# The first modulation of a seven-sublayer block, read and summed by quarters of channels, with the first sublayer's products between the quarters

## The chip, the cores and the metric

The kernel runs on one NeuronCore of a Trainium2 chip. The metric is the device time of one execution in microseconds (us). TensorE multiplies matrices, VectorE and ScalarE work on tiles, GpSimd (POOL) does a few fills and issues some transfers, SyncE (SP) issues most transfers. All arithmetic is in float32 in and out; products with weights are split into a high and a low part to keep that precision.

## The reference

One sequence of 256 tokens with 1024 channels goes through seven sublayers: for each of two layers a SwiGLU feed-forward, a mixer (mLSTM, then Mamba-2) and a second feed-forward, and at last a hybrid of block attention and short convolution. Each sublayer is modulated by a vector that is computed from a conditioning vector `c`:

```python
mod = silu(c) @ ada_w[i] + ada_b[i]            # 9 x 1024 columns per layer: shift, scale, gate of 3 sublayers
hmod = rms_norm(x, g_pre) * (1 + scale) + shift
y = rms_norm(fn(hmod), g_post)
x = x + weight * gate * y
fn = lambda h: (silu(h @ w1) * (h @ w3)) @ w2  # feed-forward, inner width 2816
```

## The kernel before

**Products.** A weight unit is a tile of 128 partitions by 1024 float32 (512 KB): two rows of blocks of 128 input channels by 512 columns, for instance. It is split on the chip: `hi` is the value rounded to the type fp32r (a copy, on ScalarE or VectorE), `lo = raw - hi` (VectorE). The modulated input is held the same way, channels on partitions, as XH and XL (8 blocks of 128 channels by 256 tokens). Each product is XH·hi + XH·lo + XL·hi, summed in PSUM. In feed-forward group 0 the input is the stationary operand and 512 weight columns move (`group_b` and `unit_b`, output tokens by columns); in groups 1 to 5 the weights are stationary and 256 tokens move (`proj_t`), and the products with w2 (`wide`) of a group follow one group later.

**The stream.** `Stream` is one ordered list of entries: weight units ("w"), rows of a modulation matrix ("ada"), sums and calls. `pump_dma` issues the loads of up to nine entries ahead of the oldest one still open (nine raw buffers), all on SyncE's queue. `step` takes the next entry: a weight unit is split into one of six hi/lo buffers; an ada entry (128 input channels by 1024 columns) is a multiply-add on VectorE, acc += raw * cs[:, k], with the conditioning value of each partition as scalar. After eight such rows the sum over partitions is taken on TensorE. Which ada entries stand between which weight units is written out in the tables GATE_AT, EARLY and COLS_AT at the top of the file, by position in a sublayer's plan (`plan_ffn`). `st.ahead` and `pieces` split some units ahead of their use. Engines run their instructions in program order.

**The start** (from the `prev = Tail(-1)` line on). ScalarE's queue loads the rows of c, the constants cC and the norm gains. SyncE's queue loads four ada rows, the first token tile of X, five ada rows, `rel` and `oh` (a small table of relative-position biases and its one-hot), then goes on with the stream; the second tile of X comes after step 5 of 8 pairs. The first modulation is 16 entries (8 blocks of k, shift and scale), 16 multiply-adds on `accC` of 128x2048, whose first row the bias `ada_b` was loaded into on POOL's queue. Between them the first token tile is normed (`x_root`, `scale_x`). Eight `bias_head` pairs (a matmul of 128x384 and a ScalarE copy into `st8`, 128 partitions wide) follow on TensorE. Then come the transposes of token tile 0 (`pre_tr`), sixteen column sums (`cols_sum`), the columns AB (`cols_set`: 1 + scale times the gain, and shift), the modulation (`affine`), and the split into XH and XL (`high`, `low`). The second token tile is normed here too, but transposed and modulated inside the first `group_b` (`between.transposes`, `between.second`), by the order list `orders[0]`. Then w1's and w3's group 0 are four units each.

`late_constants`, at position 12 of the first sublayer's plan, transposes some small rows and writes `st8` (1.5 MB) from the chip to a scratch tensor `rel_scr` in memory, which only the last sublayer reads.

Line 92 of the kernel is the helper through which every engine instruction passes, so nearly all rows carry L92 and are told apart by their tiles: accC the modulation's sums, raw the loaded tiles, hi and lo the split weights, pa the PSUM tiles of products, pb the bias heads, AB the columns, scr scratch tiles, cs the conditioning values, sil and gf the gated values of the feed-forward, py the PSUM tiles of w2.

Of the kernel before, what the change touches and what calls it, by code (L numbers as in the profile page):

```python
# [10 lines left out]
F32 = mybir.dt.float32  # L11
# [15 lines left out]
TR1_AT = 5  # L27
BY_ACT = (1, 2)
NEXT_CORE = 7
X1AT = 4  # L30
OHAT = 9

GATE_AT = [((3, 5, 7, 8), 9), ((1, 2, 3, 4), 4)] + 2 * [(range(4, 12), 11)] + [((4, 5, 6, 7), 8), (range(4, 12), 11)]
EARLY = {1: (range(12, 28, 2), 29), 4: (range(13, 29, 2), 29)}
MB_COLS = (list(range(2, 8)) + list(range(16, 26)), 26)
COLS_AT = [(range(11, 27, 2), 28), (range(5, 13), 12)] + 2 * [(range(13, 29), 29)] + [MB_COLS, (range(13, 29), 29)]


def bcast(row, n):
# [56 lines left out]
class Stream:  # L96
# [28 lines left out]
    def add_ada(self, src, info):  # L125
        self.entries.append(("ada", info, src, 1, 1024))

    def add_sum(self, srcs, fn):
# [9 lines left out]
    def pump_dma(self, n=RAW_BUFS):  # L138
        while self.dma < len(self.entries) and self.dma < min(self.open | {self.cur}) + n:
            kind, _, src, a, b = self.entries[self.dma]  # L140
            if kind in ("w", "ada"):
                raw = self.raw_pool.tile([128, 1024], F32, name="raw")
                self.nc.sync.dma_start(raw.rearrange("p (a b) -> p a b", a=a), src)
                self.raws[self.dma] = raw
            self.dma += 1

# [9 lines left out]
    def step(self, apart=False):  # L156

        if self.cur >= len(self.entries):
            return False
        kind, what, src, a, b = self.entries[self.cur]  # L160
        nc = self.nc
        self.pump_dma()
        if kind == "call":
            self.cur += 1
            what()
            return True
        raw = src if kind == "sum" else self.raws[self.cur]
        if kind == "ada":
# [82 lines left out]
def tile_blocks(ctx: ExitStack, tc, x, c, ada_w, ada_b, norm_pre, norm_post, ffn_w1, ffn_w3, ffn_w2,  # L251
# [125 lines left out]

    Gs, ABs = {}, {}

    def cols_sum(p, j):  # L380
        T.matmul(p[:, j:j + 96], accs[0][:, j * 128:(j + 1) * 128], ones[:, 0:96], start=True, stop=True)

    def cols_set(n, p):

        v = lambda t: t.rearrange("p (i h) -> p i h", h=2)
# [76 lines left out]
    def plan_hy():  # L462
# [10 lines left out]
    plans = [lambda: plan_ffn(0, 0), plan_ml, lambda: plan_ffn(0, 1), lambda: plan_ffn(1, 0),  # L473
             plan_mb, lambda: plan_ffn(1, 1), plan_hy]
# [11 lines left out]
    for n in range(n_sub):  # L486
# [15 lines left out]
    extra.setdefault(12, []).append(lambda: late_constants())  # L502
    at, last_unit = 0, {}
    for n in range(n_sub):
        for p in subs[n]:
# [200 lines left out]
            T.matmul(ps, x, w, start=first, stop=(last and kk == KT - 1 and i == len(ops) - 1))  # L706


    orders = [[(0, 1), (1, 1), (0, 6), (1, 6), (2, 1), (3, 1), (2, 6), (3, 6)]]
    orders += 7 * [[(i, 5) for i in range(4)] + [(i, 2) for i in range(4)]]  # L710

    def group_b(xh, xl, evac, between=None):

# [3 lines left out]
        if between is not None:  # L717
            for tok in range(2):
                ps = pa([128, 512])
                order = orders[-1] if tok else orders.pop(0)  # L720
                for j, (i, parts) in enumerate(order):
                    hi, lo = st.get(us[i])
                    unit_b(hi, lo, xh, xl, 2 * i, ps, tok, parts, j == len(order) - 1)
# [92 lines left out]
    def ffn(tail, between):  # L816
        with ExitStack() as es:
# [4 lines left out]
            for g in range(6):  # L822
# [5 lines left out]
                if g == 0:  # L828
                    flat = lambda t: t.rearrange("p (t c) s -> p t (c s)", t=2)
                    sb, gb = flat(sil), flat(gf)  # L830
                    group_b(XH, XL, lambda tok, p: A.activation(sb[:, tok], p, AF.Silu), between)
                    group_b(XH, XL, lambda tok, p: V.tensor_mul(gb[:, tok], p, sb[:, tok]))

                    def transposes(gb, gh, gl):
                        yield
# [768 lines left out]
    st8 = rc.tile([128, 8, 384], F32, name="st8")  # L1604
    with tc.tile_pool(name="pst", bufs=1, space=PSUM) as pst:
        crow0 = rc.tile([16, 128], F32, name="crow0")
        crow1 = rc.tile([56, 128], F32, name="crow1")
        rel = rc.tile([128, 8], F32, name="rel")
        oh = rc.tile([128, 384], F32, name="oh")
# [8 lines left out]
        V.memset(rel, 0.0)  # L1618
        V.memset(rel[32:33], -1e30)
        acc_init(0, 0)  # L1620
        st.pump_dma(4)
        load_x(0)
        st.pump_dma(OHAT)
        nc.sync.dma_start(rel[0:32], rel_bias_2)
        nc.sync.dma_start(oh, consts[:, 416:800])
        st.pump_dma()
        table(AF.Silu)
        load_rows(nc.scalar, crow1, 0, norm_pre)
# [4 lines left out]
        table(AF.Sqrt)  # L1633
        T.transpose(pc[:, 16:72], crow1, ident[:56, :56])

        def bias_head(h):
            p = pst.tile([128, 512], F32, name="pb", bufs=2)
            T.matmul(p[:, :384], rel[:, h:h + 1].to_broadcast([128, 128]), oh, start=True, stop=True)
            A.copy(st8[:, h], p[:, :384])

        for q in range(8):
            st.step()
            st.step()
            if q == 1:
                A.copy(colT[:, 16:72], pc[:, 16:72])
                P.tensor_copy(isel, cC[:, 384:416])
                P.tensor_copy(ones_r, ones)
                P.tensor_copy(pick, cs0)
                ss = x_root(0)
            if q == 2:  # L1650
                xn = scale_x(0, ss)
            if q == X1AT:
                load_x(1)
        if n_sub > 6:
            for h in range(8):
                bias_head(h)
        tr = pre_tr(0, xn)
        p = pa([128, 512])
        for j in range(16):
            cols_sum(p, j)  # L1660
        pieces("A", 2)
        cols_set(0, p[:, 0:16].rearrange("p (i h) -> p i h", h=2))
        affine(tr, 0, 0, "A", True)
        affine(tr, 0, 1, "V")
        affine(tr, 0, 0, "V")
        high(tr, 1)
        low(tr, 0)
        pieces("V", 3)
        low(tr, 1)
        pieces("A", 4)  # L1670
        ss = x_root(1)
        acc_init(0, 1)


    clock.even()
    prev.xn = scale_x(1, ss)
    table(AF.Silu)
    acc_init(1, 0)
    for t, r0, src in ((crow, 0, conv_w_2), (crow, 24, ml_norm_w), (crow, 32, mb_norm_w), (crow2, 0, mb_conv_w),
                       (crow2, 96, mb_conv_b)):  # L1680
        load_rows(nc.sync, t, r0, src)
# [59 lines left out]
```

## Time and profile before

| | |
|---|---|
| median of 3 runs | 1462.36 us (1462.06 to 1462.95) |
| the profiled execution | 1461.4 us, span 1459.6 us |
| TensorE busy | 1408.6 us (97%) |
| VectorE busy | 1224.5 us (84%) |
| ScalarE busy | 630.4 us (43%) |
| HBM read | 334.64 MB, 231 GB/s over the span |
| granted TensorE clock, mean | 0.997 |

The profile is of one execution, and its span counts from the first instruction to the last. A matmul's recorded length is its time through the array, so back-to-back matmuls start closer together than they are long: their pace is read from start to start, and lengths of merged pieces are used for that. "PEld" is the loading of stationary operands, which runs beside matmuls. A DMA's landing is counted from its issue.

### The profile page before, as it was taken

What the parts mean: (1) busy time and instruction counts of PE and PEld (TensorE: products, weight loads), DVE (VectorE), ACT (ScalarE), POOL (GpSimd) and SP (SyncE); (2) the same over time, 40 slices, a digit from 0 to 9 for tenths busy, and PEclk for the clock granted to TensorE, in tenths of its full rate; (3) what the DMA queues carried; (4) which work ended last, traced back from release to release, by engine and by line L of the source; (5) the groups of instructions that cost most, each with busy time, mean ns of one, the idle gap of its engine ahead of it and who ended that gap; (6) DMA issues with size and microseconds to landing.
All of it is one profiled execution on the core that took longest, in us unless ns stands there. A gap on an engine that the chain in (4) does not pass through costs nothing.

```text
span 1459.6 us, 24192 instructions
## 1 busy us (share of the span) xinstructions
PE 1408.6 (97%) x9476; PEld 1273.3 (87%) x9476; DVE 1224.5 (84%) x1755; ACT 630.4 (43%) x1135; POOL 36.1 (2%) x46
## 2 busy tenths in 40 slices
PE   4999999989999999999999999999999999999997
PEld 2899988867999979999889977789998799999996
DVE  7989888968888878888899999887889866879675
ACT  4433336467323254333375777652234613523112
POOL 1000000000000000000100000000000000000000
PEclk9999999999999999999999999999999999999999
DMA  9889965854878857798656574467888664566550
GB/s 375 319 319 353 327 191 179 283 198 144 284 277 288 281 165 245 249 371 305 228 196 212 145 240 139 155 216 246 303 299 300 216 194 131 145 190 202 172 173 29
DMA packets 143914, 338.85 MB, mean 232 GB/s; under 512 B 11352, under 2 KB 23224, under 8 KB 143672
## 3 DMA queue, kind: packets, MB, share of 16 engines
q1 hardware_dynamic: 142088, 332.25, 67.3%
q0 software_dynamic: 1456, 4.81, 0.9%
q8 instruction: 74, 1.21, 0.3%
q14 instruction: 40, 0.33, 0.1%
q10 hardware_dynamic: 256, 0.25, 0.0%
HBM read 334.64 MB, written 2.62 MB: 231 GB/s over the span
## 4 chain that ended last, share of the span: by engine, by line
PE 80%; DVE 11%; ACT 5%; issue 2%; DMA 1%; ACTq 0%; SPq 0%; DVEq 0%
PE pa L92 60%; PE py L92 19%; DVE scr L92 3%; DVE lo L92 3%; ACT junk L92 2%; PE cp L92 1%; DVE E L92 1%; DMA oh<-in_consts_dram 1%; PE pb L92 1%; ACT L92 1%; ACT hi L92 1%; ACT scr L92 1%; DVE accC L92 1%; DVE hi L92 0%; DVE X L92 0%
## 5 line engine op out<-in xcount | busy, mean ns | idle before, releaser
L92 DVE TENSOR_TENSOR lo<-raw,hi 128x1024 fp32r<-128x1024 f32 x453 | 546.1, 1222 | 41.0 <-ACT hi L92 28.6
L92 PE MATMUL pa<-XH,hi 128*128 128x256 f32 x2000 | 564.1, 282 | 2.4 <-ACT pad L92 1.3
L92 PE MATMUL pa<-XL,hi 128*128 128x256 f32 x2000 | 558.6, 279 | 0.0
L92 PE MATMUL pa<-XH,lo 128*128 128x256 f32 x2000 | 557.9, 279 | 0.0
L92 PEld LDWEIGHTS pa<-XH,hi 128*128 128x128 f32 x2000 | 376.0, 188 | 5.2 <-ACT pad L92 1.9
L92 PEld LDWEIGHTS pa<-XL,hi 128*128 128x128 f32 x2000 | 376.1, 188 | 1.7 <-issue 0.5
L92 PEld LDWEIGHTS pa<-XH,lo 128*128 128x128 f32 x2000 | 375.9, 188 | 0.0
L92 ACT CAST hi<-raw 128x1024 fp32r<-128x1024 f32 x271 | 275.6, 1050 | 156.7 <-PE pa L92 104.3
L92 DVE SCALAR_TENSOR_TENSOR accC<-raw,cs,accC 128x1024 f32<-128x1024 f32 x112 | 140.9, 1280 | 7.5 <-DMA accC<-in_ada_b_dram 7.5
L92 DVE CAST hi<-raw 128x1024 fp32r<-128x1024 f32 x182 | 125.6, 690 | 15.7 <-PE pa L92 15.6
L92 PE MATMUL pa<-hi,XH 128*128 128x512 f32 x320 | 125.5, 406 | 4.8 <-ACT XH L92 3.7
L92 PE MATMUL pa<-lo,XH 128*128 128x512 f32 x304 | 118.2, 395 | 0.0
L92 PE MATMUL py<-lo,gh 128*128 128x512 f32 x364 | 115.5, 396 | 0.0
L92 PE MATMUL py<-hi,gh 128*128 128x512 f32 x364 | 114.8, 397 | 0.0
L92 PE MATMUL py<-hi,gl 128*128 128x512 f32 x364 | 114.3, 395 | 0.0
L92 PE MATMUL pa<-hi,XL 128*128 128x512 f32 x320 | 95.5, 399 | 1.2 <-DVE XL L92 1.2
L92 ACT ACTIVATE sil<-pa 128x256 f32<-128x256 f32 (+1 forms) x80 | 32.3, 405 | 141.5 <-PE pa L92 141.5
L92 ACT CAST gh<-gf 128x256 fp32r<-128x256 f32 x72 | 28.0, 407 | 135.9 <-DVE gf L92 135.9
L92 PEld LDWEIGHTS py<-hi,gl 128*128 128x128 f32 x364 | 68.4, 188 | 16.3
L92 PEld LDWEIGHTS py<-lo,gh 128*128 128x128 f32 x364 | 68.4, 188 | 16.3
L92 PEld LDWEIGHTS pa<-hi,XH 128*128 128x128 f32 x320 | 60.0, 188 | 22.7 <-ACT XH L92 7.0
L92 PEld LDWEIGHTS py<-hi,gh 128*128 128x128 f32 x364 | 66.6, 188 | 14.3
(317 smaller groups left out, 1516.4 us busy)
## 6 DMA issues: line engine op xcount, KB each, us to landing
raw<-in_ffn_w_dram SPq DMA_DIRECT2D x264, 512.0 KB, 5.1
raw<-in_ada_w_dram SPq DMA_DIRECT2D x144, 512.0 KB, 5.2
raw<-in_w_in_dram SPq DMA_DIRECT2D x80, 512.0 KB, 3.7
raw<-in_mb_w_in_dram SPq DMA_DIRECT2D x41, 512.0 KB, 4.6
raw<-in_ml_w_in_dram SPq DMA_DIRECT2D x25, 512.0 KB, 4.6
raw<-in_w_ada_dram SPq DMA_DIRECT2D x24, 512.0 KB, 5.1
raw<-in_mb_w_out_dram SPq DMA_DIRECT2D x16, 512.0 KB, 4.8
raw<-in_ml_w_out_dram SPq DMA_DIRECT2D x8, 512.0 KB, 7.0
```

The costliest lines, as they stand in the source:

```text
L92: return fn(out, *args, **kw)
```

## The change

The first modulation is read as 16 entries of a new kind, "quarter": for each quarter q of 256 channels, two blocks of k at a time, shift and scale columns together, as two loads of 256 KB (runs of 1 KB) into one raw buffer. Behind the third and the fourth entry of each quarter stands one unit of w1 and of w3: the two channel blocks that this quarter's columns modulate. Both token tiles of X are loaded ahead of everything and normed together. For each quarter the multiply-adds run at half width on VectorE, except the blocks of k in ON_PE (four in the first quarter, one in the others), which are multiplied on TensorE straight into the PSUM tile `colq`; `total` adds the partition sums of accC to it, `modulate` makes the quarter's columns and XH for both token tiles in ScalarE activations of 128x256, `turn` transposes the next quarter. The products of group 0, both w1 and w3 and both token tiles, run quarter by quarter into four PSUM tiles that `ffn` then evacuates. `plan_ffn` leaves out those eight units, and the position tables of the first sublayer are moved by four. `bias_head` is gone; `late_constants` (now at position 8) makes one matmul pair of all heads (8x384) and writes the scratch tensor from 8 partitions, broadcast. `rel` and `oh` are loaded after the start.

```diff
-X1AT = 4
-OHAT = 9
-GATE_AT = [((3, 5, 7, 8), 9), ((1, 2, 3, 4), 4)] + ...
-EARLY = {1: (range(12, 28, 2), 29), 4: (range(13, 29, 2), 29)}
+ON_PE = ((4, 5, 6, 7), (7,), (7,), (7,))
+GATE_AT = [((1, 2, 3, 4), 5), ((1, 2, 3, 4), 4)] + ...
+EARLY = {1: (range(8, 24, 2), 25), 4: (range(13, 29, 2), 29)}
-COLS_AT = [(range(11, 27, 2), 28), ...
+COLS_AT = [(range(7, 23, 2), 24), ...
...
+            elif kind == "quarter":
+                raw = self.raw_pool.tile([128, 1024], F32, name="raw")
+                for j, part in enumerate(src):
+                    self.nc.sync.dma_start(raw[:, 512 * j:512 * j + 512].rearrange("p (t c) -> p t c", t=2), part)
...
-    for e in ada_entries(0, 0):
-        st.add_ada(*e)
+    for q in range(4):
+        w = ada_src(0)[0]
+        part = lambda k: w[k * 128:(k + 1) * 128, 0:2 * D].rearrange("p (t c) -> p t c", t=2)[:, :, 256 * q:256 * q + 256]
+        for i in range(4):
+            st.add_quarter([part(2 * i), part(2 * i + 1)], (lambda info, raw: macq[0](info, raw), q, 2 * i))
+            if i > 1:
+                st.add_w(*rows((ffn_w1, ffn_w3)[i - 2][0, 0], 2 * q, 2, 0, 512))
...
     def late_constants():
...
-        nc.gpsimd.dma_start(rel_scr, st8.rearrange("p h j -> p (h j)"))
+        p = pa([128, 512])
+        T.matmul(p[0:8, 0:384], rel, oh, start=True, stop=True)
+        V.tensor_copy(st8, p[0:8, 0:384])
+        nc.gpsimd.dma_start(rel_scr.rearrange("r (h j) -> h r j", h=8), st8[:, None, :].to_broadcast([8, 128, 384]))
...
+        def mac_quarter(info, raw):
+            _, q, k0 = info
+            dst = acc2[:, :, 256 * q:256 * q + 256]
+            for j in range(2):
+                k, part = k0 + j, raw[:, 512 * j:512 * j + 512]
+                if k in ON_PE[q]:
+                    for b in range(4):
+                        T.matmul(colq[:, 4 * q + b:4 * q + b + 1], part[:, 128 * b:128 * b + 128], cs[:, k:k + 1],
+                                 start=(k == ON_PE[q][0] and b == 0), stop=False, skip_group_check=True)
+                else:
+                    V.scalar_tensor_tensor(dst, part.rearrange("p (t c) -> p t c", t=2), cs[:, k:k + 1], dst,
+                                           op0=OP.mult, op1=OP.add)
...
+        def turn(q):
+            tr = trs[q] = pst.tile([128, 2, 2, 128], F32, name="tr", bufs=2)
+            for kk in range(2):
+                for t in range(2):
+                    T.transpose(tr[:, kk, t], xn[t][:, 256 * q + 128 * kk:256 * q + 128 * kk + 128], ident)
+
+        def total(q):
+            for b in range(4):
+                c0 = 256 * q + 128 * (b % 2)
+                T.matmul(colq[:, 4 * q + b:4 * q + b + 1], acc2[:, b // 2, c0:c0 + 128], ones[:, 0:1],
+                         start=False, stop=(b == 3), skip_group_check=True)
+
+        def modulate(q):
+            ks, tr = slice(2 * q, 2 * q + 2), trs[q]
+            V.scalar_tensor_tensor(ABs[0][:, ks], colq[:, 4 * q + 2:4 * q + 4], 1.0, colT[:, 16 + 2 * q:18 + 2 * q],
+                                   op0=OP.add, op1=OP.mult)
+            V.tensor_copy(ABs[0][:, 8 + 2 * q:10 + 2 * q], colq[:, 4 * q:4 * q + 2])
+            if q % 2 == 0:
+                hfs.append(scr_tile().rearrange("p (h k t) -> p h k t", h=2, k=2))
+            for dst in (XH[:, ks], hfs[-1][:, q % 2]):
+                for kk in range(2):
+                    k = 2 * q + kk
+                    A.activation(dst[:, kk], tr[:, kk].rearrange("p t s -> p (t s)"), AF.Identity,
+                                 scale=ABs[0][:, k:k + 1], bias=ABs[0][:, 8 + k:9 + k])
+
+        for i in range(6):
+            steps(1)
+            if i == 1:
+                roots = [x_root(t) for t in range(2)]
+            if i == 2:
+                xn = [scale_x(t, roots[t]) for t in range(2)]
+        turn(0)
+        total(0)
+        modulate(0)
+        steps(1)
+        for q in range(4):
+            ks, us = slice(2 * q, 2 * q + 2), st.take(2)
+            for part in (5, 2):
+                if part == 2:
+                    V.tensor_sub(XL[:, ks], hfs[-1][:, q % 2], XH[:, ks])
+                    if q < 3:
+                        steps(5)
+                        turn(q + 1)
+                    else:
+                        pieces("A", 3)
+                for w in range(2):
+                    for t in range(2):
+                        unit_b(*st.get(us[w]), XH, XL, 2 * q, ps[w, t], t, part, part == 2)
+                    if part == 2:
+                        st.done(us[w])
+            if q < 3:
+                total(q + 1)
+                modulate(q + 1)
+                if q < 2:
+                    steps(1)
+        st.pump_dma()
+        st.fixed = None
+        prev.ps = ps
+        table(AF.Silu)
         acc_init(0, 1)
```

In `unit_b`, part 5 means XH·hi and XH·lo, part 2 means XL·hi; `steps(n)` takes n entries of the stream.

## Rows read from the trace of the kernel before

**Rows 1.** The page's table of engines: busy us, share of the span, instructions.
```profile
PE 1408.6 (97%) x9476; PEld 1273.3 (87%) x9476; DVE 1224.5 (84%) x1755; ACT 630.4 (43%) x1135; POOL 36.1 (2%) x46
```

**Rows 2.** Busy time by stretch: the stretch, its length, busy time of each engine and its instructions, TensorE's granted clock (1.00 is full), the DMA engines' mean share, GB/s.
```profile
0.00:10.00 10.00, 0.58 (x2) 0.36 (x2) 1.56 (x8) 3.25 (x6) 3.20 (x9) 1.00 0.83 308
10.00:30.00 20.00, 10.95 (x42) 6.68 (x43) 19.96 (x21) 7.45 (x15) 0.00 (x0) 1.00 1.03 404
30.00:44.00 14.00, 9.68 (x51) 7.34 (x51) 11.99 (x28) 8.63 (x20) 4.59 (x5) 1.00 1.04 390
44.00:60.00 16.00, 16.00 (x70) 12.87 (x69) 14.75 (x16) 8.68 (x10) 0.00 (x0) 1.00 0.80 281
60.00:180.00 120.00, 120.00 (x880) 113.19 (x879) 106.93 (x118) 41.81 (x60) 3.29 (x4) 1.00 0.92 331
```

**Rows 3.** The chain of waits from 0 to 64 us: start, length, on what.
```profile
17.56 8.04 PE pb L92 x16
...
27.96 3.80 PE pa L92 x32
...
31.78 0.25 DVE AB L92 x2
...
40.67 22.54 PE pa L92 x112
```

**Rows 4.** VectorE in the timeline of 0 to 60 us: start, length of the merged piece, operation, count, and in brackets the idle time before it with what ended it.
```profile
8.78 4.87 DVE L92 SCALAR_TENSOR_TENSOR accC<-raw,cs,accC 128x1024 f32<-128x1024 f32 x4 [7.48 <-DMA accC<-in_ada_b_dram]
...
16.21 0.88 DVE L92 TENSOR_SCALAR scr<-X,ss 128x512 f32<-128x512 f32 x2
17.01 12.05 DVE L92 SCALAR_TENSOR_TENSOR accC<-raw,cs,accC 128x1024 f32<-128x1024 f32 x10
```

**Rows 5.** TensorE in the timelines of 0 to 60 and 50 to 84 us, same columns. A matmul of plain float32 is two passes, and passes are counted.
```profile
25.43 1.04 PE L92 MATMUL pa<-cC,scr 128*128 128x128 f32 x8
...
27.96 3.78 PE L92 MATMUL pa<-ones,accC 128*128 128x96 f32 x32 [1.49 <-issue]
...
32.63 1.54 PE L92 MATMUL pa<-hi,XH 128*128 128x512 f32 x4 [0.88 <-ACT XH L92]
...
47.17 2.03 PE L92 MATMUL pa<-hi,XL 128*128 128x512 f32 x8
...
60.24 0.28 PE L92 MATMUL pa<-XH,hi 128*128 128x256 f32 x1
```

**Rows 6.** The DMA view's packet line in three saturated stretches: 20 to 24 us (rows of the modulation, runs of 4 KB), 28 to 32 us (weights, runs of 2 KB), 176 to 180 us (weights of the last group, runs of 1 KB).
```profile
DMA packets 449, 1.64 MB, mean 410 GB/s; under 512 B 49, under 2 KB 49, under 8 KB 449
...
DMA packets 688, 1.57 MB, mean 393 GB/s; under 512 B 48, under 2 KB 48, under 8 KB 688
...
DMA packets 1404, 1.42 MB, mean 354 GB/s; under 512 B 45, under 2 KB 1396, under 8 KB 1404
```

**Rows 7.** The DMA view's issues, median us from issue to landing last, of the stretches 4 to 6, 9.9 to 19, 28 to 32 and 44 to 48 us, in this order.
```profile
X<-in_x_dram SPq DMA_DIRECT2D x1, 512.0 KB, 5.8
...
raw<-in_ada_w_dram SPq DMA_DIRECT2D x7, 512.0 KB, 8.2
...
raw<-in_ada_w_dram SPq DMA_DIRECT2D x2, 512.0 KB, 10.7
...
raw<-in_ffn_w_dram SPq DMA_DIRECT2D x1, 512.0 KB, 3.6
```

**Rows 8.** SyncE's queue in the timeline from 0 us: start, length of the merged piece, line, what is loaded, count.
```profile
4.70 0.33 SPq L1601 DMA_DIRECT2D X<-in_x_dram  x1
...
10.59 8.05 SPq L143 DMA_DIRECT2D raw<-in_ada_w_dram  x7
```

**Rows 9.** Busy time by stretch for the bias matmuls and their copies alone (passes on TensorE in brackets, then weight loads and copies; then the granted clock).
```profile
17.50:20.00 2.50, 2.44 (x4) 1.43 (x5) 0.48 (x1) 1.00 1.04 415
20.00:22.50 2.50, 2.50 (x6) 1.19 (x6) 0.96 (x2) 1.00 1.02 406
22.50:25.00 2.50, 2.50 (x8) 1.06 (x7) 1.64 (x4) 1.00 1.03 410
```

**Rows 10.** Groups of instructions by form over the whole span: operation, output and inputs with their shapes, count, busy us and mean ns of one, idle time before them.
```profile
L92 DVE TENSOR_TENSOR lo<-raw,hi 128x1024 fp32r<-128x1024 f32 x453 | 546.1, 1222 | 41.0 <-ACT hi L92 28.6
...
L92 ACT CAST hi<-raw 128x1024 fp32r<-128x1024 f32 x271 | 275.6, 1050 | 156.7 <-PE pa L92 104.3 <-PE py L92 34.3 <-issue 10.8
L92 DVE SCALAR_TENSOR_TENSOR accC<-raw,cs,accC 128x1024 f32<-128x1024 f32 x112 | 140.9, 1280 | 7.5 <-DMA accC<-in_ada_b_dram 7.5
...
L92 ACT ACT_TABLE_LOAD x40 | 51.3, 1283 | 2.8 <-issue 2.1
...
L92 ACT ACTIVATE XH<-pa,AB 128x128 fp32r<-128x128 f32 x56 | 21.1, 457 | 5.2 <-PE pa L92 3.2 <-DVE AB L92 1.9
...
L92 DVE TENSOR_TENSOR XL<-scr,XH 128x512 fp32r<-128x512 f32 x28 | 18.6, 688 | 1.6 <-ACT scr L92 1.3
...
L92 DVE SCALAR_TENSOR_TENSOR X<-scr,ss,X 128x512 f32<-128x512 f32 x24 | 17.0, 749 | 0.4
...
L92 ACT ACTIVATE scr<-pad,convT 128x256 f32<-128x256 f32 x16 | 8.8, 609 | 0.0
```

**Rows 11.** ScalarE in the timeline of 10 to 14 us: the root of the first token tile of X.
```profile
10.55 0.63 ACT L92 ACTIVATE junk<-X 128x512 bf16<-128x512 f32 x1 [1.20 <-DMA X<-in_x_dram]
...
13.81 0.29 ACT L92 ACTIVATE ss<-ss 128x1 f32<-128x1 f32 x1 [1.78 <-DVE ss L92]
```

More of the change, by code (lines that the diff above doesn't have):

```diff
@@ L29 @@
 NEXT_CORE = 7
-X1AT = 4
-OHAT = 9
-GATE_AT = [((3, 5, 7, 8), 9), ((1, 2, 3, 4), 4)] + 2 * [(range(4, 12), 11)] + [((4, 5, 6, 7), 8), (range(4, 12), 11)]
-EARLY = {1: (range(12, 28, 2), 29), 4: (range(13, 29, 2), 29)}
+ON_PE = ((4, 5, 6, 7), (7,), (7,), (7,))
+GATE_AT = [((1, 2, 3, 4), 5), ((1, 2, 3, 4), 4)] + 2 * [(range(4, 12), 11)] + [((4, 5, 6, 7), 8), (range(4, 12), 11)]
+EARLY = {1: (range(8, 24, 2), 25), 4: (range(13, 29, 2), 29)}
 MB_COLS = (list(range(2, 8)) + list(range(16, 26)), 26)
-COLS_AT = [(range(11, 27, 2), 28), (range(5, 13), 12)] + 2 * [(range(13, 29), 29)] + [MB_COLS, (range(13, 29), 29)]
+COLS_AT = [(range(7, 23, 2), 24), (range(5, 13), 12)] + 2 * [(range(13, 29), 29)] + [MB_COLS, (range(13, 29), 29)]
 def bcast(row, n):
@@ L126, in add_ada, with add_quarter @@
         self.entries.append(("ada", info, src, 1, 1024))
+    def add_quarter(self, srcs, info):
+        self.entries.append(("quarter", info, srcs, 2, 512))
     def add_sum(self, srcs, fn):
@@ L167, in step @@
         raw = src if kind == "sum" else self.raws[self.cur]
-        if kind == "ada":
+        if kind in ("ada", "quarter"):
             what[0](what, raw)
@@ L378, in tile_blocks @@
     Gs, ABs = {}, {}
-    def cols_sum(p, j):
-        T.matmul(p[:, j:j + 96], accs[0][:, j * 128:(j + 1) * 128], ones[:, 0:96], start=True, stop=True)
     def cols_set(n, p):
@@ L434, in grp, with plan_ffn @@
         return [rows(w, 0, 8, c0, n)]
-    def plan_ffn(i, j):
+    def plan_ffn(i, j, first=False):
         w1, w3, w2 = ffn_w1[i, j], ffn_w3[i, j], ffn_w2[i, j]
         ps = []
-        for g in range(6):
+        for g in range(first, 6):
             n = 512 if g < 5 else 256
@@ L471, in plan_hy @@
         return ps + [rows(w_out_2[0], 2 * k, 2, 0, D) for k in range(4)]
-    plans = [lambda: plan_ffn(0, 0), plan_ml, lambda: plan_ffn(0, 1), lambda: plan_ffn(1, 0),
+    plans = [lambda: plan_ffn(0, 0, True), plan_ml, lambda: plan_ffn(0, 1), lambda: plan_ffn(1, 0),
              plan_mb, lambda: plan_ffn(1, 1), plan_hy]
     subs = {n: plans[n]() for n in range(n_sub)}
-    for e in ada_entries(0, 0):
-        st.add_ada(*e)
+    macq = []
+    for q in range(4):
[5 more added lines that the diff above has]
+                st.add_w(*rows((ffn_w1, ffn_w3)[i - 2][0, 0], 2 * q, 2, 0, 512))
     extra, base = {}, 0
@@ L501, in tile_blocks @@
         base += ln
-    extra.setdefault(12, []).append(lambda: late_constants())
+    extra.setdefault(8, []).append(lambda: late_constants())
     at, last_unit = 0, {}
@@ L706, in unit_b @@
             T.matmul(ps, x, w, start=first, stop=(last and kk == KT - 1 and i == len(ops) - 1))
-    orders = [[(0, 1), (1, 1), (0, 6), (1, 6), (2, 1), (3, 1), (2, 6), (3, 6)]]
-    orders += 7 * [[(i, 5) for i in range(4)] + [(i, 2) for i in range(4)]]
+    order_b = [(i, 5) for i in range(4)] + [(i, 2) for i in range(4)]
     def group_b(xh, xl, evac, between=None):
@@ L719, in group_b @@
                 ps = pa([128, 512])
-                order = orders[-1] if tok else orders.pop(0)
-                for j, (i, parts) in enumerate(order):
+                for j, (i, parts) in enumerate(order_b):
                     hi, lo = st.get(us[i])
-                    unit_b(hi, lo, xh, xl, 2 * i, ps, tok, parts, j == len(order) - 1)
+                    unit_b(hi, lo, xh, xl, 2 * i, ps, tok, parts, j == len(order_b) - 1)
                     if tok and parts == 2:
@@ L830, in ffn @@
                     sb, gb = flat(sil), flat(gf)
-                    group_b(XH, XL, lambda tok, p: A.activation(sb[:, tok], p, AF.Silu), between)
-                    group_b(XH, XL, lambda tok, p: V.tensor_mul(gb[:, tok], p, sb[:, tok]))
+                    if tail.n == 0:
+                        for tok in range(2):
+                            A.activation(sb[:, tok], between.ps[0, tok], AF.Silu)
+                        for tok in range(2):
+                            V.tensor_mul(gb[:, tok], between.ps[1, tok], sb[:, tok])
+                    else:
+                        group_b(XH, XL, lambda tok, p: A.activation(sb[:, tok], p, AF.Silu), between)
+                        group_b(XH, XL, lambda tok, p: V.tensor_mul(gb[:, tok], p, sb[:, tok]))
                     def transposes(gb, gh, gl):
@@ L1603, in tile_blocks @@
     crow2 = rc.tile([120, 128], F32, name="crow2")
-    st8 = rc.tile([128, 8, 384], F32, name="st8")
+    st8 = rc.tile([8, 384], F32, name="st8")
+    rel = rc.tile([128, 8], F32, name="rel")
+    oh = rc.tile([128, 384], F32, name="oh")
     with tc.tile_pool(name="pst", bufs=1, space=PSUM) as pst:
@@ L1607, in tile_blocks @@
         crow1 = rc.tile([56, 128], F32, name="crow1")
-        rel = rc.tile([128, 8], F32, name="rel")
-        oh = rc.tile([128, 384], F32, name="oh")
         load_rows(nc.scalar, crow0, 0, c)
@@ L1620, in tile_blocks @@
         acc_init(0, 0)
-        st.pump_dma(4)
         load_x(0)
-        st.pump_dma(OHAT)
-        nc.sync.dma_start(rel[0:32], rel_bias_2)
-        nc.sync.dma_start(oh, consts[:, 416:800])
+        load_x(1)
         st.pump_dma()
@@ L1634, in tile_blocks @@
         T.transpose(pc[:, 16:72], crow1, ident[:56, :56])
[L1636 to L1671, printed above, removed]
+        colq = pst.tile([128, 512], F32, name="colq")
@@ new lines, in tile_blocks @@
+        ps = {(w, t): pa([128, 512]) for w in range(2) for t in range(2)}
+        hfs = []
+        acc2 = accs[0].rearrange("p (t c) -> p t c", t=2)
+        def mac_quarter(info, raw):
[10 more added lines that the diff above has]
+                                           op0=OP.mult, op1=OP.add)
@@ new lines, in tile_blocks, with steps @@
+        macq.append(mac_quarter)
+        A.copy(colT[:, 16:72], pc[:, 16:72])
+        P.tensor_copy(isel, cC[:, 384:416])
+        P.tensor_copy(ones_r, ones)
+        P.tensor_copy(pick, cs0)
+        st.fixed = "A"
+        ABs[0] = cst.tile([128, 16], F32, name="AB", bufs=2)
+        trs = {}
+        def steps(n):
+            for _ in range(n):
+                assert st.step()
+        def turn(q):
[3 more added lines that the diff above has]
+                    T.transpose(tr[:, kk, t], xn[t][:, 256 * q + 128 * kk:256 * q + 128 * kk + 128], ident)
@@ new lines, in tile_blocks @@
+        for i in range(6):
[16 more added lines that the diff above has]
+                        turn(q + 1)
+                    else:
+                        pieces("A", 3)
[9 more added lines that the diff above has]
+                    steps(1)
@@ L1672, in tile_blocks @@
+        st.pump_dma()
+        st.fixed = None
+        prev.ps = ps
+        table(AF.Silu)
         acc_init(0, 1)
     clock.even()
-    prev.xn = scale_x(1, ss)
-    table(AF.Silu)
     acc_init(1, 0)
+    nc.sync.dma_start(rel[0:32], rel_bias_2)
+    nc.sync.dma_start(oh, consts[:, 416:800])
     for t, r0, src in ((crow, 0, conv_w_2), (crow, 24, ml_norm_w), (crow, 32, mb_norm_w), (crow2, 0, mb_conv_w),
```

1 line of the change is left out of this document (added).

## The prediction

> **What bounds the kernel now.** I read first the page's table of engines [rows 1], then busy time by stretch [rows 2]. The execution takes 1461.4 us, its span 1459.6; the median of the runs, 1462.36, lies 0.96 above, and I add that at the end. TensorE is busy 97% of the span, but not evenly: 0.58 us of the first 10, 10.95 of the next 20, 9.68 of the 14 after those, and from 44 us on it never stops. So only the start can give much. There two others are full: the DMA engines (share 1.03 at 404 GB/s) and VectorE (19.96 of 20 us) from 10 to 30 us. The chain of waits [rows 3] says what the start waits for: its bias matmuls stand on it, but only because they fill TensorE's idle time; the column sums begin at 27.96, as the last multiply-add runs, then come the columns AB at 31.78, the modulation, the split into XH and XL, the second token tile, and from 40.67 the matmuls run unbroken. VectorE's timeline [rows 4] shows the cause of 27.96: sixteen multiply-adds, 1.21 us apart, that begin at 8.78 behind the bias row and end at 29.06. On TensorE [rows 5] the first product starts at 32.63, and group 1 of the feed-forward (the first moving operand of 256 columns) at 60.24. The 96 products of 512 columns before it need 96 x 0.233 = 22.4 us ((2.03 - 0.40) / 7 apart) and take 27.6. My sum is when group 1 can start after the change; what follows keeps its order, and TensorE covered all of 60 to 180 us with VectorE at 89% and DMA at 0.92 [rows 2], so a shift should carry through.
>
> **Transfers.** The bytes stay, but both tiles of X now come first, and the modulation comes in runs of 1 KB instead of 4. The DMA view [rows 6] has each kind in a saturated stretch: 410 GB/s for 4 KB runs, 393 for 2 KB, 354 for 1 KB. A 512 KB entry then takes 1.48 us (quarter) or 1.33 (weights). Data begin to move at about 2 us; X and the constants (1.3 MB) are through at 5.2. Sixteen quarters and eight weights add 23.7 + 10.7, so the last ends at 39.6 and is seen about 1.3 us later, 40.9. The first quarter with its weights (last w3) is seen at 6.5 + 4 x 1.48 + 2 x 1.33 = 15.1, and each later one 8.6 us after. SyncE now issues 32 halves instead of 16 whole transfers, at about 0.4 us each [rows 8], under the 0.74 us that a half moves.
>
> **First columns.** The bias row still releases VectorE at 8.78. Half-width multiply-adds: the nearest row, 128x512 on X, is 749 ns [rows 10], 0.07 less start to start, as 1280 against 1210 for whole ones; I take 0.68. Quarter 0 has four on VectorE (2.7 us), ready at 11.5. ScalarE's roots, two squares of 0.75 us and a root of 0.29 for each token tile [rows 11], run from 9.35 with VectorE's small step between, to 13.8; both scalings (four of 0.44 [rows 4], two reciprocals) end at 15.1. Then the lows of the first w1 and w3, 1.21 each: 17.5. The columns start there, by VectorE and by the landing of w3 (15.1, high 1.05, low 1.21) alike. AB takes 0.25 [rows 3], ScalarE's first modulation of 256 columns 0.6 (609 ns for 256 columns with scale and bias; 457 for 128 from PSUM gives 0.5 to 0.6 [rows 10]), so products begin at 18.45, 14.2 us earlier than now.
>
> **The loop of a quarter.** What bounds the rest is the round of engines between one quarter's columns and the next. On TensorE, in program order: sixteen products 3.73; four small matmuls of the modulation row k = 7, eight passes at 0.118 (32 in 3.78 [rows 5]), 0.95; four transposes 0.52; eight products with XL 1.87; four closing sums 0.95. That is 8.0 us. AB, one modulation and hand-offs add 1.1, in which TensorE has nothing: 9.1 us a quarter, against 8.6 for the transfers and about 8.9 on VectorE (seven half multiply-adds 4.8, two lows 2.4, XL 0.7 after its wait for ScalarE, AB 0.25). So the loop decides, narrowly.
>
> **Cold products.** The bias matmuls, after 8.9 us in which TensorE waited, ran 0.64 us a pass until about 22.3 and 0.33 to 0.42 afterwards, though the granted clock reads 1.00, the 2.4 GHz level, in all three stretches [rows 9]. The first quarter's products also come after a nearly idle stretch. Some 4.7 us at that pace would turn 3.73 into about 6: plus 2.2, which I take; ends 0 and 4. The Trainium skill (TensorE: Matmul & The Clock Gate, Part 1: The HAM clock gate) says that an idle array starts at half clock until it has been busy for a while. The pace of the passes agrees with it, the granted clock of the same rows does not. By the rule the term stays; by the granted clock alone it is nothing and the time 2.2 us lower.
>
> **The end of the start.** Columns of quarter 3 begin at 17.5 + 3 x 9.1 + 2.2 = 47.0, its products at 48.0, and end 5.6 later, 53.6. ScalarE has four modulations, three highs (0.95 apart) and a table load of 1.28 [rows 10] before the first SiLU (0.6), so the first of the four PSUM buffers comes free at 54.4: a stall of 0.8 that the old order did not have. Group 1 starts at 54.4 against 60.24: 5.8 us earlier.
>
> **The other edits.** Eight bias matmul pairs and eight ScalarE copies leave the start: they lay in TensorE's idle time, worth nothing. In their place late_constants issues one such pair later, where nothing covers it: two passes of 0.42, and its hand-over, 0.95 us on the path (0.6 to 1.5). The scratch write of 1.5 MB is now fed from 8 partitions in 1.5 KB runs instead of 128 partitions in 12 KB ones; no row shows such a transfer. Nothing reads it before the last sublayer; it competes with weights at a DMA share near 0.8 to 0.9, with up to nine entries buffered. I take 0, ends 0 and +3. On POOL's queue only later modulation-bias loads stand behind it. The two loads rel and oh and five small rows go to SyncE behind the start's transfers, long before their use: 0. The gate's multiply-adds keep their place in the stream except one pair (2.6 us of VectorE), which moves behind the start, and three units are split ahead there instead of about four. VectorE then needs some 24 us for group 1's 22.6 of TensorE, out of a lead of 8 us: 0, ends 0 and +3.8. Sum: -5.8 + 0.95 = -4.9. That makes 1456.5 in the profile and **1457.5** as a median.
>
> **Rivals.**
> (a) *Only the transfers bind.* If small matmuls overlap and nothing is cold, the last low is ready at 40.9 + 2.3 = 43.2; products then end at 49.8, group 1 starts at 50.5. Gain 9.7 - 0.95 = 8.8: 1453.5. For it: loop and transfers differ by 0.5 us a quarter. Against: the closing sums wait for XL's products in TensorE's order.
> (b) *VectorE gives it back.* The pair and the missing unit (2.6 + 1.2 us) come out as a stall in group 1: 1457.5 + 3.8 = 1461.3. For it: VectorE at 89% of 60 to 180 us. Against: three units of lead.
> (c) *Slower: halved transfers become bound by latency.* An issue at 10.59 came right at the landing of X, issued at 4.70 and landed 5.8 us later; in that queue it stands eight transfers behind X (five rows of the modulation, rel and oh lie between) [rows 7, 8]. With about eight in flight, 42 transfers in all, the last lands near 8 + 34 / 8 x latency. Half-size transfers should land faster than the 8.2 us of whole ones (3.6 in a quiet stretch [rows 7]); 7 us gives 38 and no loss. If they keep the 10.7 us of the crowded stretch, w3 is seen at 53.5, group 1 starts at 63.1, and with the late pair that is 3.8 us slower: 1466. It decides against the change above about 9.8 us. The Trainium skill (DMA: Bandwidth & Descriptors, Measured) asks for transfers of 1 MiB for three quarters of peak; its fit for one DMA (Anatomy of one DMA) gives 2.6 us for 256 KB, an estimate. Taken singly the 32 halves would last 84 us. The trace disagrees: seven whole ones were issued in 8.05 us [rows 8], 1.28 apart, so they overlap.
> (d) *The change does not do what it says*: if accC or XH is waited for as a whole, a quarter's products wait for later quarters. Against: the sums of the shift half start at 27.96 beside a multiply-add of the scale half that ends at 29.06 [rows 3, 4], so waits go by region. Its chance is in (c)'s side, under 0.03; with all 22.4 us of products behind the last low (43.2), AB and modulation (0.8) and the stall (0.8), group 1 starts at 67.2, and the time is 1462.4 + 7.0 + 0.95 = 1470.3.
>
> **How the numbers follow.** Forecast 0.5, its own range 1455.5 to 1460; (a) 0.18; (b) 0.2; (c) and (d) 0.12. The range, 1453 to 1463, leaves out (c), (d) and the far ends. A measurement of this kernel tells 0.2%, 2.9 us, from no change, so faster means below 1459.4: most of the forecast and (a), 0.67. Same (b and the forecast's upper end) 0.22; slower 0.11.
>
> **What would show it.** Right: products from about 18.5 us; columns of the four quarters some 9 us apart, with TensorE pausing about 1 us each time; last w3 landing near 41; group 1 at 53 to 56; TensorE unbroken after it. Wrong: DMA share clearly below 1 between 8 and 40 us (c); quarters over 10 us apart; pauses of TensorE between 55 and 90 us (b), or a first quarter already late because the roots or the bias row hold VectorE.

## The result and the profile after

The changed kernel takes 1475.4 us (median of 6, 1473.55 to 1479.96) against 1462.21: a ratio of 1.0096, 95% interval [1.0080, 1.0112]. It is 13 us slower where 4.9 faster was forecast, and outside the range of 1453 to 1463. The profiled execution took 1475.62 us, its span is 1473.8. Of the runs below, the profiled execution of e7 took 6830 us; it is left out, so e7 has no trace to set beside the others.

Busy time by stretch, of the changed kernel (columns as in [rows 2]):

```profile
10.00:20.00 10.00, 8.58 (x40) 8.49 (x41) 6.01 (x12) 4.35 (x10) 0.00 (x0) 1.00 1.03 341
...
40.00:50.00 10.00, 9.03 (x41) 7.46 (x42) 8.75 (x13) 3.81 (x6) 0.00 (x0) 0.83 1.00 361
50.00:60.00 10.00, 9.03 (x40) 7.34 (x39) 5.40 (x8) 8.23 (x12) 4.31 (x5) 0.83 0.78 264
...
100.00:120.00 20.00, 20.00 (x159) 18.79 (x158) 17.35 (x21) 5.37 (x10) 1.11 (x1) 1.00 0.91 264
120.00:140.00 20.00, 13.15 (x67) 10.55 (x65) 5.18 (x8) 1.71 (x3) 0.00 (x0) 0.96 0.72 135
140.00:160.00 20.00, 16.00 (x113) 15.50 (x114) 16.36 (x15) 7.41 (x10) 0.00 (x0) 0.78 0.96 353
```

Two things differ from before. From 120 to 160 us TensorE is busy 29 of 40 us, where [rows 2] had it full, and in the first half of that VectorE only 5.18 of 20: the DMA engines work (share 0.72) but move 135 GB/s. In the second half the mean granted clock is 0.78, against 1.00 before. And between 40 and 60 us it is 0.83. The chain of waits (start, length, on what) names the first:

```profile
14.99 3.57 PE colq L92 x16
...
19.52 1.51 PE colq L92 x8
...
21.99 5.68 PE pa L92 x16
...
41.52 5.54 PE pa L92 x16
...
93.83 16.31 PE pa L92 x128
...
110.15 31.91 DMA raw<-in_ffn_w_dram
```

For 32 us the chain stands on the loads of the feed-forward's weights. What occupies the DMA engines meanwhile is the scratch write of late_constants. The DMA view of the changed kernel, issues and landing from 105 to 145 us (first fence) and the two queues from 120 to 124 (second), and that write in the kernel before (third):

```profile
raw<-in_ada_w_dram SPq DMA_DIRECT2D x5, 512.0 KB, 23.2
rel_scr<-st POOLq DMA_DIRECT2D x1, 1536.0 KB, 34.1
```

```profile
q0 software_dynamic: 45, 0.21, 45.6%
q1 hardware_dynamic: 173, 0.34, 28.7%
```

```profile
rel_scr<-st POOLq DMA_DIRECT2D x1, 1536.0 KB, 9.2
```

The write lands 34.1 us after its issue instead of 9.2. In four microseconds its queue (q0) moves 0.21 MB, 52 GB/s, and its 45 packets hold 45.6% of the time of 16 engines, near what 8 engines have, so one packet of some 4.6 KB takes 0.65 us; the weight loads (q1) get 0.34 MB, 85 GB/s. A modulation row lands after 23.2 us.

The start shows no such hole. VectorE's columns of the four quarters and the first product of group 1 (the row of 60.24 in [rows 5]):

```profile
21.05 0.16 DVE L92 SCALAR_TENSOR_TENSOR AB<-colq,colT 128x2 f32<-128x2 f32 x1 [1.68 <-PE colq L92]
...
31.64 0.16 DVE L92 SCALAR_TENSOR_TENSOR AB<-colq,colT 128x2 f32<-128x2 f32 x1 [1.64 <-PE colq L92]
...
40.58 0.16 DVE L92 SCALAR_TENSOR_TENSOR AB<-colq,colT 128x2 f32<-128x2 f32 x1
...
51.02 0.16 DVE L92 SCALAR_TENSOR_TENSOR AB<-colq,colT 128x2 f32<-128x2 f32 x1 [1.50 <-PE colq L92]
```

```profile
59.21 0.28 PE L92 MATMUL pa<-XH,hi 128*128 128x256 f32 x1
```

Columns come at 21.05, 31.64, 40.58 and 51.02 (forecast 17.5, 28.8, 37.9, 47.0), group 1 at 59.21 instead of 60.24 (forecast 54.4). So the start itself gave 1.0 us, and the write took back far more.

### The profile page after: what moved, and what is told of

The parts are those of the page before. It is cut to its first block, busy times and chain, and to the rows that moved or that the text cites. A ratio compares the mean times of both kernels' runs of the same rounds, so it can differ in the third digit from the quotient of the medians.

```text
span 1473.8 us, 24304 instructions
## 1 busy us (share of the span) xinstructions
PE 1419.9 (96%) x9518; PEld 1286.7 (87%) x9518; DVE 1216.8 (83%) x1752; ACT 633.2 (43%) x1136; POOL 36.5 (2%) x46
## 4 chain that ended last, share of the span: by engine, by line
PE 76%; DVE 12%; ACT 5%; DMA 5%; issue 2%; SPq 0%; ACTq 0%; DVEq 0%
PE pa L92 57%; PE py L92 17%; DVE lo L92 4%; DVE scr L92 3%; DMA raw<-in_ffn_w_dram 3%; ACT junk L92 2%; PE cp L92 1%; DVE accC L92 1%; DMA raw<-in_ada_w_dram 1%; DVE E L92 1%; ACT hi L92 1%; PE colq L92 1%; ACT L92 1%; ACT scr L92 1%; DVE X L92 0%
## 5 line engine op out<-in xcount | busy, mean ns | idle before, releaser
L92 ACT CAST hi<-raw 128x1024 fp32r<-128x1024 f32 x274 | 279.2, 1051 | 181.5 <-PE pa L92 90.5
L92 DVE SCALAR_TENSOR_TENSOR accC<-raw,cs,accC 128x1024 f32<-128x1024 f32 (+1 forms) x121 | 140.0, 1168 | 7.6 <-DMA accC<-in_ada_b_dram 7.0
L92 PE MATMUL pa<-hi,XH 128*128 128x512 f32 x320 | 129.3, 415 | 7.8 <-ACT XH L92 6.7
L92 PE MATMUL pa<-lo,XH 128*128 128x512 f32 x304 | 121.6, 404 | 0.0
L92 PEld LDWEIGHTS pa<-hi,XH 128*128 128x128 f32 x320 | 61.8, 193 | 26.3 <-ACT XH L92 10.1
```

Of the source, the lines that this page charges most:

```text
L92: return fn(out, *args, **kw)
```

## The experiments

Two theories of where the 13 us went: **W**, the write from 8 partitions starves the loads; **S**, the start costs them. **R** is a rival inside W: not the 8 partitions but the 1024 short runs are slow. For the missing gain at the start, **C**: TensorE's clock falls or stays low; **V**: VectorE's round of a quarter decides; **T**: TensorE's does.

**e1, the write from 128 partitions.**

```diff
-        T.matmul(p[0:8, 0:384], rel, oh, start=True, stop=True)
-        V.tensor_copy(st8, p[0:8, 0:384])
+        P.tensor_copy(rel16, rel[:, None, :].to_broadcast([128, 16, 8]))
+        T.matmul(p[:, 0:384], rel16.rearrange("p r h -> p (r h)"), oh, start=True, stop=True)
+        V.tensor_copy(st8, p[:, 0:384])
+        nc.gpsimd.dma_start(bass.AP(..., ap=[[384, 128], [16 * 3072, 8], [1, 384]]), st8[:, None, :].to_broadcast([128, 8, 384]))
```

> The changed kernel, but the scratch copies are written from 128 partitions: the one matmul pair makes 16 replicas of the 8 heads (128x384), and the transfer sends each partition's run of 1.5 KB eight times. Same bytes, same 1024 runs, same queue. Theory W (the write from 8 partitions holds the DMA engines for 34 us and starves the weight loads): it lands within 12 us of its issue, TensorE stays busy from 100 to 160 us, and the time falls by 13 to 15, to 1460 to 1462.5. Rival R (1024 short runs on GpSimd's queue are what is slow): it still lands after 20 us or more, 1470 or above. Rival S (the start is what costs): unchanged, 1473 to 1476.

Measured: 1460.56 us, ratio to before 0.9987 [0.9977, 0.9996]. The write's landing, its queue in the DMA view of 111 to 115 us, and busy time by stretch with the one that had been starved:

```profile
DMA to landing us min/median/max: 9.3/9.3/9.3
```

```profile
q0 software_dynamic: 248, 1.14, 73.5%
```

```profile
40.00:50.00 10.00, 9.02 (x43) 7.38 (x42) 8.45 (x13) 3.91 (x6) 0.00 (x0) 0.83 1.01 370
50.00:60.00 10.00, 9.03 (x41) 7.38 (x41) 5.70 (x9) 8.26 (x12) 4.28 (x5) 0.83 0.77 260
60.00:100.00 40.00, 40.00 (x294) 37.71 (x293) 37.42 (x42) 15.03 (x21) 3.52 (x4) 1.00 0.87 324
100.00:120.00 20.00, 20.00 (x159) 19.14 (x158) 17.74 (x23) 6.04 (x12) 0.93 (x1) 1.00 1.00 374
120.00:140.00 20.00, 20.00 (x135) 18.22 (x134) 19.86 (x21) 7.07 (x9) 0.00 (x0) 1.00 1.01 386
140.00:160.00 20.00, 20.00 (x137) 18.39 (x136) 15.94 (x20) 7.82 (x12) 0.00 (x0) 1.00 0.82 292
```

W holds and R falls: the same 1024 runs from 128 partitions land in 9.3 us, TensorE is full again, and 14.8 us are back. S is out for the bulk. The queue's row says more: 248 packets of the same 4.6 KB take 73.5% of 16 engines' time, 0.19 us each instead of 0.65. So the write from 8 partitions was not only on fewer engines, each of its packets took over three times as long.

**e2 and e7, that part alone.** e2 is the kernel before without its bias heads at the start, with the late pair and the write from 8 partitions; e7 is e2 with the write of e1.

```diff
-        if n_sub > 6:
-            for h in range(8):
-                bias_head(h)
...
     def late_constants():
...
+        (late pair and write as in the change; in e7 as in e1)
```

> The kernel before with this one part of the change: the eight bias matmul pairs and copies leave the start, late_constants makes one pair (8x384) and writes the scratch copies from 8 partitions. Theory W: about 1462.2 + 1 (the late pair) + 13 to 15 = 1476 to 1478, with TensorE starved for some 15 us after the write's issue. Rivals R and W agree here. Rival S: 1462 to 1464.

> The kernel before without its eight bias matmul pairs at the start; one late pair and the wide write in their place. Theory C (those matmuls, in TensorE's idle time, kept its clock up for the column sums and the first products): column sums in 6.0 us instead of 3.8, group 1 at 64 us instead of 60.2, and 1462.4 + 3.8 + 0.6 = 1466 to 1467.5. Rival (they cost nothing and gave nothing, as the forecast had it): 1462 to 1463.5. Against e2 (1481.0) it also prices the write from 8 partitions alone: 14 to 15 us by theory W.

Measured: e2 1481.0 us, ratio 1.0124 [1.0109, 1.0139]; e7 1466.1 (nine executions from 1463.4 to 1466.7), ratio 1.0025 [1.0015, 1.0034]. The difference, 14.9 us, is the write alone, as in e1 (e2 and e7 ran on different chips; each set against its own runs of the kernel before, the difference is 14.2). But e2 was 3 us above what W allowed, and e7 explains it: without the bias heads the old kernel is some 3.6 us slower by that ratio (4.4 by the medians), the late pair included. TensorE in e2's timeline, and e2's busy time from 40 to 50 us:

```profile
28.02 5.98 PE L92 MATMUL pa<-ones,accC 128*128 128x96 f32 x32 [9.23 <-issue]
```

```profile
64.08 0.28 PE L92 MATMUL pa<-XH,hi 128*128 128x256 f32 x1
```

```profile
40.00:50.00 10.00, 7.74 (x31) 6.26 (x30) 7.75 (x18) 5.45 (x10) 0.00 (x0) 0.83 0.62 223
```

After 9.2 us of waiting the column sums take 5.98 us instead of the 3.78 of [rows 5], and group 1 starts at 64.08 instead of 60.24. From 40 to 50 us the granted clock is 0.83, where the kernel before has 1.00. The bias matmuls, in time that TensorE had to spare, had brought it to full pace. That is read from e2; of e7 only the time is known.

**e4, products in the pauses** (on top of e1):

```diff
                 total(q + 1)
+                for _ in range(4):
+                    nc.tensor.matmul(pc, ones_r, XH[:, 0:2].rearrange("p k s -> p (k s)"), start=True, stop=True)
                 modulate(q + 1)
```

> The wide write of e1, and four extra products of 512 columns, whose result nobody reads, behind each of the three closing sums, where TensorE pauses for 1 us. Theory C (the pauses let the granted clock fall to half from 42.8 to 46.2 and from 53 to 56.4): the clock stays at 1.00 from 25 to 60 us, the sixteen products of quarters 2 and 3 take 3.7 us each instead of 5.5 and 5.4, and group 1 starts some 3.5 us earlier than in e1. Rival: the clock falls all the same, or the extra products only add 0 to 2.8 us.

Measured: 1458.14 us, ratio 0.9968 [0.9955, 0.9981]; 2.4 below e1: its five runs lie between 1457.69 and 1458.27, e1's ten between 1458.95 and 1462.15. Clock and first product of group 1:

```profile
40.00:50.00 10.00, 10.00 (x55) 8.01 (x54) 8.71 (x15) 4.24 (x7) 0.71 (x1) 1.00 0.98 363
50.00:60.00 10.00, 9.66 (x57) 7.97 (x56) 7.78 (x9) 7.74 (x13) 3.57 (x5) 1.00 0.91 306
```

```profile
56.39 0.39 PE L92 MATMUL pa<-XH,hi 128*128 128x256 f32 x1 [0.34 <-ACT sil L92]
```

The granted clock stays at 1.00 where e1 has 0.83, and group 1 starts at 56.39 instead of 58.90. C holds for the later quarters, with 2.5 us of the expected 3.5.

**e5 and e8, no modulation row on TensorE** (`ON_PE = ((), (), (), ())`; e5 on e1, e8 on e6, whose three extra pairs become twelve: ten before the first entry and two ahead of the first closing sums).

> The wide write of e1, and no row of the modulation multiplied on TensorE: all 32 half-width multiply-adds on VectorE (7 more than in the change: 4 in quarter 0, 1 in each other). Theory T (TensorE's round decides the loop, and its small passes at half clock delay the first columns): first columns no later than 21 us, quarters 9 to 10 apart, group 1 within 1 us of e1 or earlier. Rival V (VectorE then decides): quarter 0 gains 3.1 us of multiply-adds and each other 0.8, group 1 starts 2 to 5 us later than in e1.

> e6 with no row of the modulation multiplied on TensorE, and twelve extra passes' pairs ahead of the first sums in their place. If VectorE decides the loop once TensorE runs at full clock (rival V of e5), quarters are 9.7 us apart as in e5 and it is 1 to 3 us slower than e6. If TensorE's round still decides, it is as fast as e6 or up to 1 us faster.

Measured: e5 1460.21 us, ratio 0.9989 [0.9980, 0.9999]; e8 1459.54, 0.9984 [0.9975, 0.9993]. e5's time cannot be told from e1's, and its trace has the signs of T, not the price of V: first columns at 20.83, quarters 9.7 to 9.9 apart, and group 1 not 2 to 5 us later than e1's 58.90 but earlier (though in quarters 2 and 3 its columns wait for VectorE alone):

```profile
57.31 0.38 PE L92 MATMUL pa<-XH,hi 128*128 128x256 f32 x1 [0.33 <-ACT sil L92]
```

e8 is 0.7 us slower than e6, between its two forecasts, so its trace has to decide. Its columns of the quarters, and two rows of TensorE behind them:

```profile
20.43 0.16 DVE L92 SCALAR_TENSOR_TENSOR AB<-colq,colT 128x2 f32<-128x2 f32 x1 [0.66 <-PE colq L92]
...
30.17 0.16 DVE L92 SCALAR_TENSOR_TENSOR AB<-colq,colT 128x2 f32<-128x2 f32 x1
...
39.90 0.16 DVE L92 SCALAR_TENSOR_TENSOR AB<-colq,colT 128x2 f32<-128x2 f32 x1
...
49.63 0.16 DVE L92 SCALAR_TENSOR_TENSOR AB<-colq,colT 128x2 f32<-128x2 f32 x1
```

```profile
21.71 0.40 PE L92 MATMUL pa<-lo,XH 128*128 128x512 f32 x1
...
25.21 0.60 PE L92 MATMUL tr<-cC,scr 128*128 128x128 f32 x4
```

With twelve extra pairs ahead the first sixteen products run 0.233 apart (fifteen of them from 21.71 to 25.21), but the quarters are 9.73 us apart and, from the second on, the columns wait for nothing but VectorE: with all 32 multiply-adds it decides. So the rows on TensorE in quarters 1 to 3 should pay once its clock is up, which e9 tests.

**e6, extra pairs ahead with quarter 0's rows kept on TensorE** (on top of e4):

```diff
+        def extra(n):
+            for _ in range(n):
+                nc.tensor.matmul(ps[1, 1][:, 0:384], ident, cC[:, 0:384], start=True, stop=True)
+
+        extra(2)
         for i in range(6):
             steps(1)
+            if i == 2:
+                extra(1)
...
```

> e4 (wide write, extra products in the three pauses) with three extra pairs of 128x384 passes before the first columns as well: two behind the transposes of the small rows, one between the two groups of small products of quarter 0. Their result is not read. Theory C: the small products of quarter 0 take 1.9 us instead of 3.6 from the second group on, the sixteen products of quarter 0 take 3.7 instead of 5.7, and group 1 starts 2 to 3 us earlier than in e4 (56.4): about 1455.5 to 1456.5. Rival V: VectorE and the landings then hold the columns, the loop stays at 9 us from lows that come no earlier, and the time is that of e4, 1457.5 to 1458.5.

Measured: 1458.85 us, ratio 0.9980 [0.9972, 0.9989]: nothing beyond e4, with group 1 at 56.99. The small products and two of the large ones:

```profile
10.36 3.41 PE L92 MATMUL colq<-cs,raw 128*128 128x1 f32 x16
...
15.05 3.41 PE L92 MATMUL colq<-cs,raw 128*128 128x1 f32 x16
...
22.91 0.63 PE L92 MATMUL pa<-hi,XH 128*128 128x512 f32 x1
...
26.33 0.51 PE L92 MATMUL pa<-hi,XH 128*128 128x512 f32 x1
```

TensorE was busy without a break from 7.6 to 20.9 us, and yet the small products took 3.41 us for 16 passes and the large ones ran 0.43 apart until 26.3. These three wide pairs and the products with one moving column did not bring the pace up; the twelve wide pairs of e8, without those products, did.

e6 also settles what held the first columns. Its w3 of quarter 0 was split from 15.23, 1.8 us earlier than in the changed kernel, and still the columns came only at 20.95, after VectorE had waited 3.42 us for TensorE. So the time lies near the rival's, but not for its reason, and theory C missed because the three pairs did not raise the pace.

**e9, both**: e8 with `ON_PE = ((), (7,), (7,), (7,))`.

> The wide write, the extra products in the pauses, the twelve extra pairs ahead of the first sums, and the modulation's rows on TensorE only in quarters 1 to 3 (block k = 7), none in quarter 0. Theory: first columns near 20.4 us as in e8, first sixteen products at full clock (3.7 us), quarters 9.0 us apart as in e4 instead of 9.7 as in e8, so columns of quarter 3 near 47.5, group 1 at 54.5 and 1455.5 to 1456.5, below e4 (1458.1) and the kernel before. Rival: the small products lower the clock again or VectorE and the landings hold the loop, group 1 at 56 to 57 as in e4, e6 and e8, 1457.5 to 1459.

Measured: 1456.6 us (1455.54 to 1457.77), ratio 0.9957 [0.9943, 0.9970], the lowest median of all: 5.7 us below the kernel before. (Its interval overlaps with e4's, and it ran on another chip.)

```profile
20.87 0.16 DVE L92 SCALAR_TENSOR_TENSOR AB<-colq,colT 128x2 f32<-128x2 f32 x1
...
29.82 0.16 DVE L92 SCALAR_TENSOR_TENSOR AB<-colq,colT 128x2 f32<-128x2 f32 x1
...
38.76 0.16 DVE L92 SCALAR_TENSOR_TENSOR AB<-colq,colT 128x2 f32<-128x2 f32 x1
...
47.70 0.16 DVE L92 SCALAR_TENSOR_TENSOR AB<-colq,colT 128x2 f32<-128x2 f32 x1
```

```profile
54.84 0.39 PE L92 MATMUL pa<-XH,hi 128*128 128x256 f32 x1 [0.35 <-ACT sil L92]
```

Quarters are 8.94 us apart, group 1 starts at 54.84, and from the second quarter on the columns wait for VectorE alone. One multiply-add a quarter less on VectorE than in e8 made the round 0.79 us shorter, so it is VectorE that sets it.

## Why the prediction was wrong

**The step that failed** is in "the other edits": "The scratch write of 1.5 MB is now fed from 8 partitions ... I take 0, ends 0 and +3". It measured 14.8 us (the change less e1) and 14.9 (e2 less e7). I counted on the nine buffered entries to cover the write and let the missing row stand for a small number; none of the four rivals had this term. The runs show that the source's eight partitions set the pace (34 us against 9 from 128 partitions with the same runs), and that the write does not only last: while it runs, the weight loads come down to 85 GB/s. TensorE asks for some 300 in that stretch ([rows 2]: 331). Nine buffers are 4.7 MB, about 14 us at that pace, and the hole is longer. TensorE then stands still for 10.9 of the 40 us from 120 to 160; the other 4 or so (an estimate, 14.8 less that) fit the low clock of 140 to 160. That the loads wait because they need the engines that the write holds is the reading that fits; no row names the engine of a packet.

**The bias heads "worth nothing"** was the second error: without them the old order is about 3.6 us slower (e7, interval 2.2 to 5.0), the late pair included. That the first quarter of the new order lacks them in the same way is an argument; e8's wide passes ahead of it, and the pace behind them, speak for it.

**First columns**, forecast 17.5, came at 21.05: 3.6 of the 4.8 us by which the start fell short (the three rounds added 0.5, what follows the last columns 0.8). My sum for them had VectorE and the landing of w3, and no term for TensorE at all. There 16 small passes took 3.57 us at the low pace, twice, and transposes and closing sums queued behind the second group until 21.03. The w3 of quarter 0 was split from 17.07, two microseconds later than my sum had it landing, but its low ended at 19.4 and so did not decide, as e6 shows.

**The loop** was right in size at full clock, not in kind: 9.1 forecast, 8.94 between quarters 1 and 2 and in all of e9. But there the columns wait for VectorE's lows and not for TensorE, whose round I had called the one that decides; that the two rounds are nearly as long made the number come out, by luck. VectorE's half-width multiply-adds came 0.78 apart (3.11 for four), not 0.68. At the low pace TensorE did decide, and the rounds took 10.6 and 10.4. I had put cold products into quarter 0 alone (2.2; measured 1.7, 5.5 for the sixteen against 3.8 in quarter 1). The granted clock fell again at 42.8 and at 53.0, each time after a pause of 1 us, and the sixteen products of quarters 2 and 3 took 5.4 each:

```profile
42.00:44.00 2.00, 2.00 (x8) 1.63 (x7) 1.38 (x3) 2.00 (x4) 0.00 (x0) 0.70 1.01 354
44.00:46.00 2.00, 2.00 (x6) 1.59 (x5) 1.89 (x4) 0.71 (x1) 0.00 (x0) 0.50 1.05 397
```

The Trainium skill (TensorE: Matmul & The Clock Gate, HAM oscillation — how this bites in real kernels) puts the danger in long waits for data between groups of matmuls; here pauses of 1 us came before the fall, in a stretch where TensorE was busy 9.03 of 10 us. The measurement decides: with those pauses filled, e4's clock stayed up.

**Right:** the transfers (halves and weights together moved 341 to 361 GB/s from 10 to 40 us; my terms of 1.48 and 1.33 come to 366), so rival (c) falls: the halves landed in 7.2 us (median of 8 to 40 us), and I had 7 as harmless. Rival (a) falls, since TensorE and then VectorE decide and not the transfers. Rival (b) falls too: in e1 TensorE is full from 60 to 100 us. Rival (d) falls: products began at 21.99, and quarter 1's second weight unit was split only from 25.81. The late pair: e1's group 1 starts 1.34 us earlier than before and its span is 0.8 shorter, so all that comes later costs 0.5, where I had 0.95 (one execution of each, so no more than a hint). The end of the sum, group 1 at 54.4 and 1457.5, was reached by e9 (54.84 and 1456.6), which has what the change lacked: a write from all partitions, a clock that stays up, and no modulation rows on TensorE in quarter 0. It got there by other terms, first columns 3.4 us later and no cold products, so its agreement does not confirm the sum.

**Open:** why eight engines moved only 52 GB/s. That it were eight fits the share of 45.6%; the Trainium skill (DMA: Bandwidth & Descriptors, Why a DMA increments its semaphore by 16 and not by 1) has a transfer spread over no more engines than divide the outermost dimension of both its sides, here 8, and the trace agrees so far. But eight engines at e1's 0.19 us for a packet would have moved 1.5 MB in some 8 us (an estimate from e1's row), so the number of engines is the smaller part; why a packet from these partitions took 0.65 us, no run shows. e1 also sends each partition's run 8 times instead of 128, and the two are not told apart. Open too is whether the same write from another queue would be as slow, which was not tried.

What exactly lets the clock fall is not settled either. In e4, e6 and e9 it stayed up with the pauses filled. But the same pause of 1 us before quarter 1 of the changed kernel was followed by no fall, and e8's clock fell although its pauses were filled, after VectorE had kept TensorE waiting for 1.40 us:

```profile
30.00:40.00 10.00, 10.00 (x43) 7.87 (x43) 9.19 (x16) 3.91 (x6) 0.00 (x0) 0.83 1.08 360
```

## What to carry to other kernels

Before moving a transfer, count the partitions on its chip side: a write of 1.5 MB that nobody waits for can cost 15 us when few partitions feed it, because loads that somebody does wait for crawl while it runs. Where no row shows a transfer of that shape, its bytes do not bound its price: give the term a wide upper end, or measure it alone first. And idle-time matmuls are not free to remove: look at the pace of what runs next after them.

## What the hardware showed that was not expected

- The scratch write: 1.5 MB from 8 partitions 34.1 us, from 128 partitions with the same 1.5 KB runs 9.3, with 12 KB runs 9.2. A packet of 4.6 KB took 0.65 us from 8 partitions, 0.19 from 128.
- Small products (one moving column) ran at 0.22 us a pass in the first quarter, at 0.21 in e6 when TensorE had been busy for 7 us before them, at 0.10 in the later quarters; wide passes in their place brought the next products to 0.233 apart (e8).
- At the very start the granted clock reads 1.00 although matmuls run at half pace; after its first recorded fall it agrees with them (0.50 in 44 to 46 us of the changed kernel, products 0.43 apart).
